# A conditioning group placed inside the norm ahead of the FFN of a hybrid decoder block, with a retuned table of places

## The chip, the cores and the metric

The kernel runs on one core of a Trainium2 chip, in float32 throughout. The metric is the device time of one execution in microseconds (us). A time of 1207.5 us is the median of three runs of the kernel before.

## The reference, cut to what matters

One decoder block for 256 tokens of width 2048. A vector `c` gives, through the matrix `w_ada` (2048 x 12288, 96 MB), six vectors of 2048 numbers ("adaLN"): a shift, a scale and a gate for the mixer (SH1, SC1, G1) and the same for the FFN (SH2, SC2, G2).

```python
mod = silu(c) @ w_ada + b_ada
sh1, sc1, g1, sh2, sc2, g2 = split(mod, 6)
h = modulate(rms_norm(x, norm1_g), sh1, sc1)            # h * (1 + scale) + shift
q, k, v, gb, gc, xt = split(h @ w_in, ...)              # 2048 x 6144
attn = attention(rms_norm(q), rms_norm(k), v)           # 8 heads, causal
conv = gb * causal_dwconv(gc * xt)                      # 3 taps
mixed = concat(rms_norm(attn), rms_norm(conv))
x = x + g1 * (mixed @ w_out)                            # 2048 x 2048
h2 = modulate(rms_norm(x, norm2_g), sh2, sc2)           # the norm ahead of the FFN
u_gate, u_up = split(causal_dwconv(h2 @ w_ffn_up), 2)   # 2048 x 11264
x = x + g2 * ((silu(u_gate) * u_up) @ w_ffn_down)       # 5632 x 2048
```

## The kernel before

**Matrices.** Every weight matrix is streamed in tiles of 1 MB (128 x 2048 floats) through five buffers, `raw`. SyncE issues the loads in a fixed order, the next one each time a buffer is given back (`load_next`). TensorE multiplies float32 by a split: ScalarE writes the rounded part `hi` of a tile (L225), VectorE the rest `lo` = raw - hi (L231), both with three buffers, and TensorE makes three products for each piece (hi with both parts of the activations, lo with one).

**Slots.** The program is a list of slots, one for each weight tile: 0 to 47 input projection, 48 to 63 output projection, from 64 (`N_OUT`) FFN up and down. In slot i the main loop at the end of the kernel issues, in program order: the split of the tile two slots ahead, the side work hung on the slot with `at(i, f, ...)` (a class number decides whether it stands before or behind the `lo` part, and a list `hi_late` whether the `hi` part stands before or behind it), the products of the slot, and then the `w_ada` tiles listed for the slot in `extra`. Each engine runs its instructions in this order; nothing is reordered later. `CFG` is the table of all these places.

**adaLN.** A group `[part, first chunk, width, on TensorE, first slot, span]` of `CFG['ada']` is a block of columns of `w_ada`. `Ada.consume` takes one 1 MB tile of it: on VectorE four or so multiply-adds (L287), or on TensorE (`pe` True) 16 matmuls a tile in four column quarters at once, which the profile counts in records of L281; a group of 512 columns has four tiles. Then `evac` copies the sum (ScalarE, L298), and `cols` turns it by four transposes (L314) into columns of the scale `A2` or the shift `B2`. Part 3 is SH2. Its chunks 8 to 11 are taken on TensorE in slot 63, all four tiles behind the last product of the output projection.

**The end of the mixer and the norm.** `evac_c(3)` adds the last quarter of the output projection to the residual x (VectorE, L454 and L456, twice: once for each 128 tokens). `tr_out(f)` turns the quarter f of the new x by eight transposes on TensorE (L489) and two copies on ScalarE (L492) into `x1T`. `norm2` squares the last quarter (ScalarE, L531, twice), makes the root of the mean (VectorE, ScalarE), writes the reciprocal into a diagonal `n2d` (VectorE, L537), spreads it over all partitions by one product with ones (`n2b`, TensorE, L539), copies it (L541) and makes from `x1T` the first eight chunks of h2 (VectorE L557, ScalarE L559, VectorE L562). `ss_part` sums the squares of the first three quarters (L498, L499, and a small root `pre`, L500, on ScalarE). The first FFN products (L662 with hi, L666 with lo) wait for the first chunk of h2.

**The start.** `ffn_cols` turns five small vectors by five transposes on TensorE (L167) and five copies on VectorE (L169), in slot 2.

Of the kernel before, what the change touches and what calls it, by code (L numbers as in the profile page):

```python
# [28 lines left out]

CFG = {'ada': [[3, 12, 512, False, 51, 12], [3, 0, 512, True, 58, 5], [0, 2, 256, False, 0, 7],
# [5 lines left out]
 'bufs': [43, 10, 5, 3, 2],  # L38
# [3 lines left out]
 'split': [4, 8],  # L42
 'segs': [8, 5, 5, 4],
 'heads': [35, 38, 38, 36, 41, 45, 43, 41],
 'head_steps': [1, 1, 2, 3, 4],
 'conv': [[1, 2, 1, 5, 4, 5, 7, 9], [2, 3, 3, 3, 2, 3, 2, 6]],
 'qk': [[1, 6], [2, 7]],
 'norms': [50, 55],
 'x1': 52,
 'fcols': 2,  # L50
 'hold': [1, 2, 0],
 'evac': [4, 0, 1],
 'sq': [4, 6, 2],
 'tr': [6, 7, 3],
 'part': 1,
 'up': [[1, 4], [1, 3], [0, 0], [2, 2]],
 'gate': [-21, -14, -2, -9],
 'cls': {'add': 0,
         'h2_rest': -1,
         'att_n': 1,  # L60
         'qk_norm': 0,
         'out_norm': -1,
         'cols': 0,
         'conv_q': -1,
         'att_q': 0,
         'up_gate': 2,
         'hold_a': 0,
         'spread': 1,
         'conv_m': 2,
         'ffn_cols': 2,  # L70
         'h_chunks': -1,
# [15 lines left out]
         'gate_down': 1,
         'conv_g': 0,
         'conv_c': 2,
         'evac_in': 0,  # L90
         'qk_root': 2,
         'evac_out': 1},
 'la': 2,
 'h_act': True,
 'h_lag': 1,
 'hi_late': [2, 3, 5, 6, 7, 8, 10, 12, 13, 15, 18, 27, 42, 44, 49, 50, 52, 53, 54, 56, 57, 63, 67, 68, 70, 75, 76,
# [3 lines left out]


@with_exitstack
def tile_block(
# [24 lines left out]
    def small(n, name):  # L128
        return sb.tile([P, n], F32, tag="small", bufs=16, name=name, padded_shape=[P, 32])
# [20 lines left out]
    vc, _ = rows("vc", [(by_p(c[0]), 16)])  # L150
# [212 lines left out]
    SLICES = [(0, 2), (2, 4), (4, 8), (8, 16)]  # L363

    def halves(v):
        return v[:, :256], v[:, 256:]
# [11 lines left out]
            mm(o, b, hi[:, k], start=False, stop=(last and k == nk - 1))  # L378

    def evac_in(f):  # L380
        for t in range(2):
# [17 lines left out]
    turns = []
    for (ka, kb), order in zip(SLICES, CFG["orders"]):  # L400
        if kb - ka == 2:
            turns += [((w + "0", w + "1"), ka, True, True) for w in order]
        else:
            turns += [((f,), k, k == ka, k + 4 == kb) for f in order for k in range(ka, kb, 4)]
    uses = {}
    for i, (fs, *_) in enumerate(turns):
        for f in fs:
            uses.setdefault(f, []).append(i)
    for i, (fs, k, first, last) in enumerate(turns):
        def near(f, d):  # L410
            u = uses[f]
            n = u.index(i) + d
            return 0 <= n < len(u) and abs(u[n] - i) <= 2

        def go(hi, lo, fs=fs, k=k, new=[not near(f, -1) for f in fs], end=[not near(f, 1) for f in fs]):
            m = 4 // len(fs)
            for h, f in enumerate(fs):
                mm_tok(f, hi[:, h::len(fs)], lo[:, h::len(fs)], [halves(hT[k + j]) for j in range(m)], m, new[h], end[h])

        slots.append((pair_load(k, fs[0]) if len(fs) == 2 else w_load(w_in, k, 4, [(COL[fs[0]] * 512, 512)]), 4, go))  # L420
        for f in fs:
            if not near(f, 1):
                at(len(slots), evac_in, f)
            if i == uses[f][-1]:
                at(len(slots), done.add, f)
                in_last[f] = len(slots)
    N_IN = len(slots)

# [466 lines left out]

# [148 lines left out]
    for i in range(len(slots)):  # L1044
        more = i + LA < len(slots)
        hi_late = i == N_OUT or i in CFG["hi_late"]
        if more and not hi_late:
            split_hi(slots[i + LA][1])
        todo = sorted(tasks.pop(i, []), key=lambda e: e[0])
# [12 lines left out]
        for g, r in extra.get(i, []):  # L1062
            g.consume(r)
# [33 lines left out]
```

## Time and profile before

| | |
|---|---|
| median of 3 runs (lowest to highest) | 1207.5 us (1207.37 to 1208.13) |
| the profiled execution | 1208.13 us, its span 1206.3 us |
| TensorE (PE) busy | 1174.2 us, 97% of the span |
| VectorE (DVE) busy | 916.8 us, 76% |
| ScalarE (ACT) busy | 616.9 us, 51% |
| bytes moved | 313.78 MB, 260 GB/s over the span |
| mean granted TensorE clock | 0.996 of full |

PE is the engine to look at: the span less its busy time is 32.1 us. Of the span, 87% of the chain of work that ended last is PE's own. The profiled execution is the slowest of the three, 0.63 us over their median.

### The profile page before, as it was taken

To read this page: it belongs to the slowest core of one execution; us is meant where nothing else is said; L and a number is where in the kernel's file an instruction comes from. 1 tells how busy PE (TensorE), PEld (TensorE's weight loads), DVE (VectorE), ACT (ScalarE), POOL (GpSimd) and SP (SyncE) were. 2 spreads that over 40 slices of the span, in tenths; PEclk is the share of its full clock that TensorE was granted. 3 is DMA by queue.
4 is the path that set the end of the run, shared out by engine and by line. 5 is a ranking of instruction groups with operands and counts; after the bars stand their busy time and mean duration, and the time that the engine had idled before them with its cause. 6 is when DMAs were issued, how large, how long until landed. Compare 5 with 4: busy or idle time off the path is not lost.

```text
span 1206.3 us, 15491 instructions
## 1 busy us (share of the span) xinstructions
PE 1174.2 (97%) x6041; PEld 965.1 (80%) x6041; DVE 916.8 (76%) x1099; ACT 616.9 (51%) x852; POOL 1.6 (0%) x9
## 2 busy tenths in 40 slices
PE   5899999999999998999999999999999999999998
PEld 3677788877777776888888888888888888888886
DVE  2789999997789896778888687766755667666776
ACT  5554347465765445555555344555434555345452
POOL 0000000000000000000000000000000000000000
PEclk9999999999999998999999999999999999999999
DMA  9999997999779997655576799554565564664542
GB/s 363 358 373 378 362 389 277 367 349 349 261 238 395 360 368 260 233 179 179 201 264 238 279 345 362 199 188 162 174 230 189 168 208 149 209 225 159 176 139 105
DMA packets 194925, 313.78 MB, mean 260 GB/s; under 512 B 6650, under 2 KB 105500, under 8 KB 194596
## 3 DMA queue, kind: packets, MB, share of 16 engines
q1 hardware_dynamic: 194160, 312.52, 72.8%
q8 instruction: 47, 0.77, 0.2%
q10 hardware_dynamic: 692, 0.28, 0.1%
q14 instruction: 26, 0.21, 0.0%
HBM read 310.67 MB, written 2.10 MB: 259 GB/s over the span
## 4 chain that ended last, share of the span: by engine, by line
PE 87%; DVE 6%; ACT 3%; DMA 2%; issue 1%; SPq 0%; ACTq 0%
PE z L662 27%; PE z L666 14%; DVE lo L231 2%; DVE ada L287 2%; PE ada L281 2%; DMA raw<-in_w_ada_dram 2%; ACT hi L225 2%; PE mk L376 1%; PE mq L376 1%; PE mq L378 1%; PE mq L377 1%; PE mk L377 1%; PE mk L378 1%; PE mg L376 1%; PE mg L378 1%; PE mg L377 1%
## 5 line engine op out<-in xcount | busy, mean ns | idle before, releaser
L231 DVE TENSOR_TENSOR lo<-raw,hi 128x2048 fp32r<-128x2048 f32 (+2 forms) x204 | 449.1, 2206 | 173.0 <-ACT hi L225 166.4
L225 ACT ACTIVATE hi<-raw 128x2048 fp32r<-128x2048 f32 (+2 forms) x204 | 376.1, 1847 | 344.9 <-PE z L662 104.7
L662 PE MATMUL z<-h,hi 128*128 128x512 f32 x1408 | 382.6, 396 | 2.1 <-DVE h L562 2.1
L662 PEld LDWEIGHTS z<-h,hi 128*128 128x128 f32 x1408 | 243.1, 189 | 37.8 <-issue 3.3
L666 PEld LDWEIGHTS z<-h,lo 128*128 128x128 f32 x1408 | 213.1, 189 | 27.9
L666 PE MATMUL z<-h,lo 128*128 128x256 f32 x1408 | 220.7, 281 | 0.0
L287 DVE SCALAR_TENSOR_TENSOR ada<-raw,csil,ada 128x1024 f32<-128x1024 f32 (+2 forms) x165 | 159.4, 968 | 4.5 <-DMA raw<-in_w_ada_dram 0.5
L579 DVE TENSOR_TENSOR ub<-z,ub 128x256 f32<-128x256 f32 x104 | 37.5, 417 | 33.0 <-ACT ub L576 33.0
L593 ACT ACTIVATE uy<-ub,fc,fc 128x256 f32<-128x256 f32 x88 | 45.7, 591 | 5.5 <-DVE uy L600 5.5
L281 PE MATMUL ada<-raw,crep 128*32 128x512 f32 (+1 forms) x320 | 37.1, 569 | 9.5 <-DMA raw<-in_w_ada_dram 9.5
L600 DVE SCALAR_TENSOR_TENSOR uy<-ub,fc,uy 128x254 f32<-128x254 f32 x88 | 42.5, 483 | 3.1
L609 ACT ACTIVATE gh<-uy 128x512 fp32r<-128x512 f32 x22 | 13.9, 632 | 58.1 <-DVE uy L607 58.1
L598 DVE SCALAR_TENSOR_TENSOR uy<-ub,fc,uy 128x255 f32<-128x255 f32 x88 | 42.1, 479 | 1.5 <-ACT uy L593 1.5
L576 ACT ACTIVATE ub<-z 128x256 f32<-128x256 f32 x104 | 33.1, 381 | 19.4 <-PE z L662 19.4
L603 ACT ACTIVATE uy<-uy 128x512 f32<-128x512 f32 x22 | 13.9, 631 | 44.7 <-DVE uy L600 44.7
L281 PEld LDWEIGHTS ada<-raw,crep 128*32 128x32 f32 x320 | 8.3, 116 | 25.6 <-issue 12.8
L376 PE MATMUL mc<-hi,h 128*128 128x512 f32 x64 | 26.0, 406 | 2.4 <-ACT pa_k L385 2.4
L610 DVE TENSOR_TENSOR gl<-uy,gh 128x512 fp32r<-128x512 f32 x22 | 15.2, 692 | 15.4 <-ACT gh L609 15.4
L376 PE MATMUL mg<-hi,h 128*128 128x512 f32 x64 | 26.1, 408 | 0.8 <-DVE v1c L169 0.8
L376 PE MATMUL mk<-hi,h 128*128 128x512 f32 x64 | 25.3, 396 | 0.7 <-ACT h L735 0.7
L378 PE MATMUL mv<-hi,h 128*128 128x512 f32 x64 | 25.0, 391 | 0.8 <-DVE h L738 0.8
L376 PE MATMUL mx<-hi,h 128*128 128x512 f32 x64 | 25.7, 401 | 0.0
(541 smaller groups left out, 1860.7 us busy)
## 6 DMA issues: line engine op xcount, KB each, us to landing
raw<-in_w_ada_dram SPq DMA_DIRECT2D x96, 1024.0 KB
raw<-in_w_ffn_up_dram SPq DMA_DIRECT2D x176, 512.0 KB
raw<-in_w_in_dram SPq DMA_DIRECT2D x48, 1024.0 KB
raw<-in_w_ffn_down_dram SPq DMA_DIRECT2D x24, 1024.0 KB
raw<-in_w_ffn_down_dram SPq DMA_DIRECT2D x24, 768.0 KB
raw<-in_w_out_dram SPq DMA_DIRECT2D x16, 1024.0 KB
xr<-in_x_dram SPq DMA_DIRECT2D x2, 1024.0 KB
x<-in_x_dram SPq DMA_DIRECT2D x8, 256.0 KB
```

What stands on the lines that cost most here:

```text
L225: act(hi[:, :nk], t[:, :nk], AF.Copy)
L231: V.tensor_tensor(out=lo[:, :nk], in0=t[:, :nk], in1=hi[:, :nk].bitcast(F32), op=ALU.subtract)
L281: mm(self.acc[q:q + 32, :], crep[:, i, :], t[:, j, :], start=(r == 0 and j < 4), stop=(r == self.tiles - 1 and j >= self.rows - 4), tile_p ...
L287: V.scalar_tensor_tensor(out=self.acc, in0=t[:, j, :], scalar=csil[:, i:i + 1], in1=self.acc, op0=ALU.mult, op1=ALU.add)
L376: mm(o, a, hi[:, k], start=(first and k == 0), stop=False)
L378: mm(o, b, hi[:, k], start=False, stop=(last and k == nk - 1))
L579: V.tensor_tensor(out=d, in0=zp[grp][ft][:, :256], in1=d, op=ALU.add)
L593: act(y, b, AF.Identity, bias=fcols[3][:, i:i + 1], scale=fcols[2][:, i:i + 1])
L598: V.scalar_tensor_tensor(out=y[:, 1:], in0=b[:, :255], scalar=fcols[1][:, i:i + 1], in1=y[:, 1:], op0=ALU.mult, op1=ALU.add)
L600: V.scalar_tensor_tensor(out=y[:, 2:], in0=b[:, :254], scalar=fcols[0][:, i:i + 1], in1=y[:, 2:], op0=ALU.mult, op1=ALU.add)
L662: mm(zp[grp][ft], hi[:, j, ft * P:(ft + 1) * P], h2T[k + j], start=k + j == ks[0], stop=k + j == ks[1] - 1)
L666: mm(zp[grp][ft][:, :256], lo[:, j, ft * P:(ft + 1) * P], h2T[k + j][:, :256], start=False, stop=False)
```

## The change

Three things. The group SH2, chunks 8 to 11, leaves the list of slots: three of its tiles are now consumed at the start of `norm2`, the fourth behind the product `n2b`, and its `evac` and `cols` go to slots 65 and 66. `tr_out(3)` moves from slot 64 to slot 65. And the table is retuned in many places: among them `ffn_cols` from slot 2 to 3, the second tile of the group `[1, 2]` from slot 2 to 3, the group `[4, 0]` from slots 49 and 50 to 49 alone, the group `[3, 0]` from slots 58 to 61 to 58 and 59, `ss_part` one slot earlier, and the FFN's side work (`gate`, `up`, the classes). The amount of work on each engine and the bytes are the same.

```diff
-         [4, 0, 512, True, 49, 2], ... [3, 8, 512, True, 63, 1],
-CFG = {'ada': [... [3, 0, 512, True, 58, 5], ... [1, 2, 256, True, 0, 4],
+CFG = {'ada': [... [3, 0, 512, True, 58, 2], ... [1, 2, 256, True, 0, 6],
+         [4, 0, 512, True, 49, 1], ...
+ 'fill': [[3, 8]],
+ 'fill_at': [0, 3, 1],
+ 'tr3': 1,
- 'fcols': 2,
+ 'fcols': 3,
- 'part': 1,
+ 'part': 0,
...
     def norm2():
-        assert {"tr0", "tr1", "tr2", "tr3"} <= done
+        assert {"tr0", "tr1", "ev3"} <= done
         m, q, r = small(2, "n2m"), small(2, "n2q"), small(2, "n2r")
+        for g, i in fill_a:
+            g.consume(i)
         for t in range(2):
             act(t2k("x1s"), x1[t, 3], AF.Square, accum_out=q[:, t:t + 1])
...
         p = bank("n2b")
         mm(p[:, :256], ones, d, start=True, stop=True)
+        for g, i in fill_b:
+            g.consume(i)
         rB.append(t1k("rB"))
...
     at(N_OUT, evac_c, 3)
-    at(N_OUT, tr_out, 3)
+    at(N_OUT + CFG["tr3"], tr_out, 3)
     at(N_OUT, norm2)
...
+    fill = []
+    for part, c0 in CFG["fill"]:
+        g = Ada(part, c0, 512, True)
+        fill += [(g, r) for r in range(g.tiles)]
+    n0, n1, n2 = CFG["fill_at"]
+    extra.setdefault(N_OUT - 1, []).extend(fill[:n0])
+    fill_a, fill_b = fill[n0:n0 + n1], fill[n0 + n1:n0 + n1 + n2]
...
     for i in range(len(slots)):
+        if i == N_OUT:
+            consume += [("a", g, r) for g, r in fill_a + fill_b]
         if i + LA < len(slots):
             consume.append(("w", i + LA))
```

The new lines shift the numbers of the file: L281, L376, L489, L531, L539, L662 before are L286, L380, L496, L540, L548, L673 in the changed kernel.

**TensorE at the norm.** Before, from the last product of the output projection to the first FFN product (`m('C', 3)1` is the last accumulator of that projection, `x1t` the turned x, `z` the FFN's accumulators; `x16` stands for 16 matmuls):

```order
L378 MATMUL m('C', 3)1_3687<-hi,mix_3071 128x512
L281 MATMUL ada_8_3789<-raw,crep 32x512 x16
L489 MATMUL x1t_3823<-ident,x_03_3202 128x128
L489 MATMUL x1t_3823<-ident,x_13_3210 128x128
...
L539 MATMUL n2b<-n2d,ones 128x256
L662 MATMUL z_0_3905<-h_0_3859,hi 128x512
```

and now, to the transposes behind the products of slot 64:

```order
L382 MATMUL m('C', 3)1_3727<-hi,mix_3088 128x512
L286 MATMUL ada_8_3798<-raw,crep 32x512 x12
L548 MATMUL n2b<-n2d,ones 128x256
L286 MATMUL ada_8_3798<-raw,crep 32x512 x4
L673 MATMUL z_0_3889<-h_0_3845,hi 128x512
...
L677 MATMUL z_3_3892<-h_3_3859,lo 128x256
L496 MATMUL x1t_3927<-ident,x_03_3270 128x128
```

The 16 matmuls of the group are now 12 ahead of `n2b` and 4 behind it, and the eight transposes stand behind 32 FFN products.

**ScalarE at the norm.** Before, from the split of tile 65 to the copy of `n2b` (`pre` is the small root, `x1T` the turned x, `x1s` the squares):

```order
L225 ACTIVATE hi<-raw 128x2048
L500 ACTIVATE pre<-ss_94 128x2
L492 ACTIVATE x1T_3828<-x1t_3823 128x512
L492 ACTIVATE x1T_3835<-x1t_3830 128x512
L531 ACTIVATE x1s,n2q<-x_03_3202 128x512
L531 ACTIVATE x1s,n2q<-x_13_3210 128x512
L533 ACTIVATE n2q<-n2m 128x2
L541 ACTIVATE rB<-n2b 128x256
```

and now:

```order
L507 ACTIVATE pre<-ss_94 128x2
L230 ACTIVATE hi<-raw 128x2048
L540 ACTIVATE x1s,n2q<-x_03_3270 128x512
L540 ACTIVATE x1s,n2q<-x_13_3278 128x512
L542 ACTIVATE n2q<-n2m 128x2
L552 ACTIVATE rB<-n2b 128x256
```

The two copies of the turned x no longer stand ahead of the squares; they come after the eight chunks of h2 and two splits.

**TensorE at slots 2 and 3.** Before, at the start of slot 2 (`pv_...` are the transposes of `ffn_cols`, `mc` and `mg` accumulators of the input projection):

```order
L378 MATMUL mc_380<-hi,h_255 128x512
L167 MATMUL pv_v1c<-ident,v_279 128x66
L167 MATMUL pv_fc_411<-ident,vf_287 128x88
L167 MATMUL pv_fc_415<-ident,vf_289 128x88
L167 MATMUL pv_fc_419<-ident,vf_291 128x88
L167 MATMUL pv_fc_423<-ident,vf_293 128x88
L376 MATMUL mg_427<-hi,h_251 128x512
```

and now, at the start of slot 3 (`mx` is the next accumulator):

```order
L382 MATMUL mg_422<-hi,h_255 128x512
L172 MATMUL pv_v1c<-ident,v_279 128x66
L172 MATMUL pv_fc_460<-ident,vf_287 128x88
L172 MATMUL pv_fc_464<-ident,vf_289 128x88
L172 MATMUL pv_fc_468<-ident,vf_291 128x88
L172 MATMUL pv_fc_472<-ident,vf_293 128x88
L380 MATMUL mx_476<-hi,h_251 128x512
```

The five transposes stand 24 products later, where a pass of the group `[1, 2]` stood before.

## Rows read from the trace of the kernel before

**Rows 1.** The page, first part: busy time of each engine, its share of the span, and its instructions.

```profile
PE 1174.2 (97%) x6041; PEld 965.1 (80%) x6041; DVE 916.8 (76%) x1099; ACT 616.9 (51%) x852; POOL 1.6 (0%) x9
```

**Rows 2.** Stretches of the span: from and to (us), length, busy time and instructions of PE, PEld, DVE, ACT and POOL, then the granted TensorE clock (1.00 is 2.4 GHz, 0.50 is 1.2 GHz), the DMA engines' share and GB/s.

```profile
0.00:30.00 30.00, 15.74 (x114) 9.85 (x115) 8.96 (x24) 16.40 (x24) 1.60 (x9) 1.00 0.97 363
...
100.00:250.00 150.00, 150.00 (x688) 120.58 (x687) 139.25 (x142) 75.60 (x144) 0.00 (x0) 1.00 0.94 351
...
450.00:462.00 12.00, 6.08 (x45) 2.33 (x43) 5.16 (x15) 3.79 (x10) 0.00 (x0) 0.87 1.02 354
...
600.00:900.00 300.00, 300.00 (x1521) 254.28 (x1520) 216.16 (x211) 143.75 (x149) 0.00 (x0) 1.00 0.70 245
900.00:1200.00 300.00, 300.00 (x1586) 257.61 (x1585) 201.56 (x223) 139.01 (x148) 0.00 (x0) 1.00 0.52 175
```

**Rows 3.** What PE's matmuls waited for, over the span: us in total, times, longest.

```profile
PE ada L281 <- DMA raw<-in_w_ada_dram: 9.5, 4, 6.9
...
PE n2b L539 <- DVE n2d L537: 3.8, 1, 3.8
...
PE z L662 <- DVE h L562: 2.1, 1, 2.1
...
PE mg L376 <- DVE v1c L169: 0.8, 1, 0.8
...
PE ssC L868 <- DVE sq L864: 0.7, 1, 0.7
```

**Rows 4.** The norm ahead of the FFN in order of time, all engines: start, duration, engine, line, operation, and in brackets the idle time before it and what ended it.

```profile
446.99 2.29 DVE L231 TENSOR_TENSOR lo<-raw,hi 128x2048 fp32r<-128x2048 f32 x1 [0.71 <-ACT hi L225]
...
449.91 0.39 PE L378 MATMUL m('C', 3)1_3687<-hi,mix 128*128 128x512 f32 x1
450.22 3.64 PE L281 MATMUL ada<-raw,crep 128*32 128x512 f32 x32
...
451.63 0.69 DVE L456 TENSOR_TENSOR x<-z,x 128x512 f32<-128x512 f32 x1
...
453.80 1.09 PE L489 MATMUL x1t<-ident,x 128*128 128x128 f32 x8
454.49 1.09 ACT L492 ACTIVATE x1T<-x1t 128x512 f32<-128x512 f32 x2 [4.70 <-PE x1t L489]
455.46 0.63 ACT L531 ACTIVATE x1s<-x 128x512 f32<-128x512 f32 x1
...
456.07 0.63 ACT L531 ACTIVATE x1s<-x 128x512 f32<-128x512 f32 x1
...
458.04 0.48 DVE L537 TENSOR_SCALAR n2d<-ident,n2r 128x128 f32<-128x128 f32 x2
...
458.67 1.08 PE L539 MATMUL n2b<-n2d,ones 128*128 128x256 f32 x2 [3.78 <-DVE n2d L537]
459.78 0.38 ACT L541 ACTIVATE rB<-n2b 128x256 f32<-128x256 f32 x1 [2.56 <-PE n2b L539]
...
461.89 2.05 PE L662 MATMUL z<-h,hi 128*128 128x512 f32 x4 [2.14 <-DVE h L562]
...
469.27 0.60 PE L314 MATMUL adac<-ident,adae 128*128 128x128 f32 x4
```

**Rows 5.** Shorter stretches, with the columns of rows 2.

```profile
42.40:45.80 3.40, 3.40 (x13) 2.72 (x12) 2.34 (x2) 3.29 (x5) 0.00 (x0) 0.50 1.07 392
...
270.00:275.00 5.00, 3.79 (x26) 2.40 (x23) 3.23 (x7) 0.83 (x1) 0.00 (x0) 1.00 1.04 399
...
458.80:461.90 3.10, 0.96 (x3) 0.27 (x3) 1.52 (x4) 1.29 (x3) 0.00 (x0) 0.50 1.07 389
461.90:465.60 3.70, 3.70 (x11) 3.12 (x12) 3.70 (x11) 2.32 (x5) 0.00 (x0) 0.50 0.93 328
465.60:469.20 3.60, 3.60 (x23) 3.17 (x22) 1.62 (x5) 3.23 (x5) 0.00 (x0) 1.00 0.01 3
```

**Rows 6.** PE alone in a stretch of the FFN, two rows of the same piece of work in neighbouring slots (columns of rows 4).

```profile
624.47 1.09 PE L662 MATMUL z<-h,hi 128*128 128x512 f32 x4
...
630.09 1.09 PE L662 MATMUL z<-h,hi 128*128 128x512 f32 x4
```

**Rows 7.** PE alone at four of its waits (columns of rows 4; the first is the wait ahead of the half clock near 42 us).

```profile
40.87 0.50 PE L376 MATMUL mc<-hi,h 128*128 128x512 f32 x1 [2.41 <-ACT pa_k L385]
...
48.77 0.50 PE L376 MATMUL mg<-hi,h 128*128 128x512 f32 x1 [0.83 <-DVE v1c L169]
...
72.82 0.50 PE L378 MATMUL mv<-hi,h 128*128 128x512 f32 x1 [0.82 <-DVE h L738]
...
271.57 1.06 PE L281 MATMUL ada<-raw,crep 128*32 128x512 f32 x8 [1.21 <-DMA raw<-in_w_ada_dram]
```

**Rows 8.** VectorE at the start, in order of time: a split, the copies of `ffn_cols` behind the first, and the chunk of h that PE waits for at 72.82.

```profile
46.29 2.29 DVE L231 TENSOR_TENSOR lo<-raw,hi 128x2048 fp32r<-128x2048 f32 x1 [1.55 <-ACT hi L225]
...
48.63 0.71 DVE L169 COPY fc<-pv_fc 128x88 f32<-128x88 f32 x4
...
72.34 0.76 DVE L738 TENSOR_TENSOR h<-hf,h 128x256 fp32r<-128x256 f32 x2
```

**Rows 9.** Slot 49: the two loads of SyncE and the two `w_ada` tiles of PE, in order of time.

```profile
355.87 3.89 SPq L258 DMA_DIRECT2D raw<-in_w_ada_dram  x2
358.27 1.92 PE L281 MATMUL ada<-raw,crep 128*32 128x512 f32 x16
```

More of the change, by code (lines that the diff above doesn't have):

```diff
@@ L28 @@
 SH1, SC1, G1, SH2, SC2, G2 = range(6)
-CFG = {'ada': [[3, 12, 512, False, 51, 12], [3, 0, 512, True, 58, 5], [0, 2, 256, False, 0, 7],
[5 rows of a table removed]
- 'bufs': [43, 10, 5, 3, 2],
[3 rows of a table removed]
+CFG = {'ada': [[3, 12, 512, False, 51, 12], [3, 0, 512, True, 58, 2], [2, 0, 1024, False, 24, 17],
[4 rows of a table added]
+ 'bufs': [43, 10, 5, 3, 2],
[6 rows of a table added]
+ 'fill': [[3, 8]],
+ 'fill_at': [0, 3, 1],
+ 'tr3': 1,
  'split': [4, 8],
  'segs': [8, 5, 5, 4],
- 'heads': [35, 38, 38, 36, 41, 45, 43, 41],
+ 'heads': [1, 4, 4, 2, 0, 4, 3, 0],
  'head_steps': [1, 1, 2, 3, 4],
- 'conv': [[1, 2, 1, 5, 4, 5, 7, 9], [2, 3, 3, 3, 2, 3, 2, 6]],
- 'qk': [[1, 6], [2, 7]],
+ 'conv': [[1, 2, 2, 5, 4, 6, 7, 8], [2, 3, 3, 3, 2, 3, 2, 6]],
+ 'qk': [[2, 6], [0, 7]],
  'norms': [50, 55],
- 'x1': 52,
- 'fcols': 2,
[L51 to L54, printed above, removed]
- 'part': 1,
[L56 to L59, printed above, removed]
+ 'x1': 54,
+ 'fcols': 3,
+ 'hold': [3, 2, 0],
+ 'evac': [4, 0, 0],
+ 'sq': [4, 6, 0],
+ 'tr': [5, 6, 1],
+ 'part': 0,
+ 'up': [[1, 3], [1, 3], [0, 0], [2, 2]],
+ 'gate': [-21, -14, -2, -11],
+ 'cls': {'add': 2,
+         'h2_rest': 0,
          'att_n': 1,
          'qk_norm': 0,
-         'out_norm': -1,
-         'cols': 0,
-         'conv_q': -1,
+         'out_norm': 0,
+         'cols': -1,
+         'conv_q': 1,
          'att_q': 0,
@@ L67 @@
          'hold_a': 0,
-         'spread': 1,
+         'spread': 2,
          'conv_m': 2,
@@ L77 @@
          'ss_part': 2,
-         'up_sum': -1,
+         'up_sum': 0,
          'sq_out': 1,
          'att_s': -1,
-         'tr_out': 0,
+         'tr_out': 1,
          'evac': 1,
          'qk_stat': 0,
-         'load_x': 2,
+         'load_x': 0,
          'att_t': 1,
          'att_o': 2,
-         'gate_down': 1,
+         'gate_down': 2,
          'conv_g': 0,
@@ L90 @@
          'evac_in': 0,
-         'qk_root': 2,
+         'qk_root': 0,
          'evac_out': 1},
@@ L95 @@
  'h_lag': 1,
- 'hi_late': [2, 3, 5, 6, 7, 8, 10, 12, 13, 15, 18, 27, 42, 44, 49, 50, 52, 53, 54, 56, 57, 63, 67, 68, 70, 75, 76,
[3 rows of a table removed]
+ 'hi_late': [2, 3, 4, 5, 6, 7, 8, 10, 12, 15, 18, 19, 27, 31, 42, 44, 49, 50, 52, 53, 54, 56, 57, 63, 67, 70, 71,
[3 rows of a table added]
 @with_exitstack
@@ L351, in tile_block @@
     done = set()
+    now = [0]
     hT = {}
@@ L361, in tile_block @@
            "x0": 10, "x1": 11}
-    SLICES = [(0, 2), (2, 4), (4, 8), (8, 16)]
     def halves(v):
@@ L380, in evac_in @@
     def evac_in(f):
+        if in_last.get(f) == now[0]:
+            done.add(f)
         for t in range(2):
@@ L396, in pair_load @@
         return issue
[L399 to L404, printed above, removed]
+    turns, upto = [], {}
+    for f, ka, kb in CFG["turns"]:
+        fs, step = ((f,), 4) if f in COL else ((f + "0", f + "1"), 2)
+        for g in fs:
+            assert upto.get(g, 0) == ka
+            upto[g] = kb
+        turns += [(fs, k) for k in range(ka, kb, step)]
+    assert len(upto) == 12 and set(upto.values()) == {16}
     uses = {}
-    for i, (fs, *_) in enumerate(turns):
+    for i, (fs, _) in enumerate(turns):
         for f in fs:
             uses.setdefault(f, []).append(i)
-    for i, (fs, k, first, last) in enumerate(turns):
+    for i, (fs, k) in enumerate(turns):
         def near(f, d):
@@ L424, in tile_block @@
             if i == uses[f][-1]:
-                at(len(slots), done.add, f)
                 in_last[f] = len(slots)
@@ L738, in h_chunks @@
                 V.tensor_tensor(out=hT[k][:, 256:], in0=ts[k], in1=hT[k][:, :256].bitcast(F32), op=ALU.subtract)
+    fill = []
[5 more added lines that the diff above has]
+    fill_a, fill_b = fill[n0:n0 + n1], fill[n0 + n1:n0 + n1 + n2]
+    for i, (g, r) in enumerate(fill):
+        if i >= n0 + n1 + n2:
+            extra.setdefault(N_OUT + (i - n0 - n1 - n2) // 2, []).append((g, r))
+        if r == g.tiles - 1:
+            a = N_OUT + 1 + max(0, (i - n0 - n1 - n2) // 2)
+            at(a, g.evac)
+            at(a + 1, g.cols)
+            ready_at.update({(g.part, g.c0 + k): a + 1 for k in range(4)})
     for part, c0, n, pe, a, span in CFG["ada"]:
@@ L888, in tile_block @@
         at(i + CFG["qk"][half][1], qk_norm, half)
+        n = i + CFG["qk"][half][1]
         for j in range(4):
@@ L891, in tile_block @@
             for i, f in zip([0] + CFG["head_steps"], (att_t, att_s, att_n, att_p, att_o, att_q)):
-                at(CFG["heads"][h] + i, f, h)
+                at(n + CFG["heads"][h] + i, f, h)
     at(CFG["norms"][0], out_norm, "A", ssA)
@@ L947, in tile_block @@
     for half in range(2):
-        xl, gl = in_last[f"x{half}"], in_last[f"g{half}"]
+        xl, gl = max(in_last[f"x{half}"], in_last[f"c{half}"]), in_last[f"g{half}"]
         o = CFG["conv"][half]
-        at(max(xl, in_last[f"c{half}"]) + o[0], conv_p, half)
+        at(xl + o[0], conv_p, half)
         at(xl + o[1], conv_c, half, 0)
@@ L1048, in tile_block @@
             split_hi(slots[i + LA][1])
+        now[0] = i
         todo = sorted(tasks.pop(i, []), key=lambda e: e[0])
```

24 rows, old and new, of the table CFG are left out of this document.

## The prediction

> **What bounds the kernel now.** I read the busy times first. TensorE (PE) works 1174.2 us of a span of 1206.3 us [rows 1]: 32.1 us without work are all that an order of instructions can win from waits, and what it loses shows there too. Next, where those 32.1 us lie. The table of stretches [rows 2] shows 14.26 us ahead of 30 us (30.00 less 15.74), when the first weights are still coming, 5.92 us at 450 to 462, and none at 100 to 250 and 600 to 1200. VectorE is at 139.25 of 150 us and the DMA engines at 0.94 in 100 to 250; at 600 to 1200 both have room. The list of PE's waits [rows 3] gives the names: `w_ada` tiles 9.5 us, 6.9 of it in one wait at the start, the product `n2b` 3.8 us, the first FFN product `z` 2.1 us, and pieces of 0.7 to 0.8 us for `mg`, `mv` and `ssC` [rows 3, 7]. Last the norm in order of time [rows 4], where the two large waits in the middle of the kernel stand next to each other.
>
> **The norm, step by step.** The last product of the output projection starts at 449.91 and ends at 450.30. PE then has the four adaLN tiles, 3.64 us, and the eight transposes, 1.09 us, to 454.89. VectorE has the last quarter of x ready at 452.32 (451.63 and 0.69), but ScalarE stands in front of the transposes: its queue holds the two copies of the turned x ahead of the squares, so it sits idle 4.70 us until PE has turned x, copies for 1.09 us, and squares at 455.46 and 456.07 [rows 4]. From the second square to `n2b` it is 2.60 us (456.07 to 458.67), from `n2b` to `z` 3.22 us (to 461.89).
>
> In the changed order no copy stands ahead of the squares. The second square can start when x is ready, at 452.32 and a handing over of some 0.15 us (`n2d` ends at 458.52, `n2b` starts at 458.67). `ss_part`, two small VectorE instructions, has moved ahead of the split of tile 65, and of the earlier ScalarE copies two are gone from the front of that split, so VectorE may come to x a little sooner: between 0 and 0.45 us, since the second half of x can't be begun before 450.30. I take 0.3. Then the second square starts at 452.2, `n2b` at 454.8, `z` at 458.0 with the durations of now. At 2.4 GHz `n2b` takes half of its 1.08 us, so `z` is at 457.5. That is 4.4 us earlier than 461.89; 3.6 us is the lower bound (no help from VectorE, `n2b` as slow as now), 4.6 the upper.
>
> The tiles cost PE no time here: 12 of 16 matmuls are three quarters of 3.64, so 2.73 us to 452.95; the fourth tile, 0.91 us, starts behind `n2b` at 455.3 and ends at 456.2, ahead of `z`. At half clock it would end near 457.7, still ahead of a `z` at 458.0. That cover is 0.3 to 1.3 us; were it gone, `z` would be late by what the tile overruns. The transposes, hidden now, are no longer: they stand behind slot 64's products, where PE has work, and cost their 1.09 us, a little less without the 0.1 us or so of start-up: 1.0. Their two copies on ScalarE come behind eight chunks of h2 and two splits, and only the chunks 12 to 15 of h2, wanted slots later, need them. Each consumed tile frees a buffer and lets SyncE issue one load; the fourth is freed some 2.3 us later than now (456.2 for 453.86). At 465.6 to 469.2 the DMA engines are at 0.01 [rows 5]: loads wait there for buffers and there is 3.6 us of room. So waits less moved work: 4.4 less 1.0, 3.4 us (2.6 to 3.6).
>
> **The clock.** The granted clock is 0.50 at 458.80 to 465.60, that is 1.2 GHz, after the idle time of 3.78 us [rows 4, 5]. Slot 64 takes 7.38 us from `z` to `adac` (461.89 to 469.27); an FFN slot at 2.4 GHz takes 5.62 us (624.47 to 630.09) [rows 6]. So the slow clock costs 1.76 us of products today. In the changed kernel PE idles 1.8 us ahead of `n2b` (452.95 to 454.8) and 1.2 to 1.3 us ahead of `z`. The trace has a wait of 2.41 us, at 40.87, behind which the clock was 0.50 for 3.40 us (42.40 to 45.80), and one of 1.21 us, at 271.57, in a stretch of 1.00 [rows 5, 7]. The new gaps lie between, but there are two of them with little between, so I take one short fall: the 3.40 us of the shorter case, of which part falls on the waits and the tile and some 2 us on products, which costs 1.0 us. Bounds: no fall, 0; a fall wholly on products, 1.7. Gain from the clock: 1.76 less 1.0, so 0.8 (0 to 1.8). The norm gives 3.4 and 0.8: 4.2 us (2.6 to 5.4).
>
> A rule speaks against taking the group apart. The Trainium skill, "Perfetto Trace Analysis", section Matmul Optimizations, says that matmuls should run back-to-back in batches, because the engine scales its power with its use; and "TensorE: Matmul & The Clock Gate", section HAM oscillation, says that idle time between bursts puts the array back to half its clock. By it the pieces ahead of and behind `n2b` don't hold the clock, and the total is that of my forecast; by the 1.21 us row alone it would be that of the first rival. The trace agrees for 2.41 and 3.78 us, and not for 1.21.
>
> **The start.** The transposes and copies of `ffn_cols` leave slot 2. PE waits 0.83 us for the first copy at 48.77 [rows 7]; that wait is gone, since a slot later VectorE's split is not in front of anything that PE needs at once. The transposes ran in the half-clock stretch of 42.40 to 45.80; now products fill it, so nothing is won there. VectorE gives the five copies, some 0.9 us (48.63 and 0.71 is their larger part), a later place. The next meeting is at 72.82, where PE waits 0.82 us for a chunk of h that VectorE makes at 72.34 [rows 7, 8]. The copies still lie ahead of it, but VectorE had idle time ahead of its split at 46.29, 1.55 us, so it may come 0 to 1.0 us sooner. Behind it, PE at 150.00 of 150 would keep a lead, but VectorE and DMA are nearly full [rows 2], and at 271.57 PE waits 1.21 us for a `w_ada` tile: a lead that the loads don't share is lost there. I take 0.4 us (0 to 1.0).
>
> **The other places.** Group `[4, 0]`: four tiles in slot 49. Two of them took 1.92 us (358.27), so the third is wanted at 360.2 and the last near 361. SyncE issued two loads at 355.87 over 3.89 us [rows 9]: the later tile's load depends on a buffer freed just before. A wait of 0 to 0.7 us, since its load is already under way; I take 0.2. Group `[3, 0]` has two tiles in slots 58 and 59 each, again the load of the third behind the use of the first: 0 to 1.0, I take 0.2. `ssC` waits 0.7 us for a square; some of VectorE's work ahead of it stands elsewhere: a gain of 0 to 0.4, I take 0.2. The tile of `[1, 2]` a slot later, heads, convolution, `evac` and `gate` places and the classes move work of VectorE and ScalarE at places where PE shows no wait (100 to 250 and 600 to 1200); the cover is the third `hi`/`lo` buffer and, at 900 to 1200, an idle VectorE for 98 of 300 us and an idle ScalarE for 161 [rows 2]. They cost nothing unless a split comes more than about a slot, 5.62 us, late. Sum of this part: -0.2 us (-1.7 to 0.4).
>
> **The sum.** 4.2, 0.4 and -0.2 are 4.4 us. The profiled execution took 1208.13, which gives 1203.7 us; it is 0.63 above the median of 1207.5, and against the median the sum is 1203.1 us.
>
> **Rivals.** (1) The clock doesn't fall: the 1.21 us row speaks for it, two gaps in a row against it. It adds 1.0 to the gain: 1202.1 us. (2) New waits on loads take part of it: the doubled tiles at slots 49, 58 and 59 at their upper bounds, 1.7 us, with no gain at `ssC` and none kept from the start; PE's longest wait for a tile in the middle of the kernel, 1.21 us, shows that such loads do come late. 4.2 less 1.7: 1205.0. (3) The change doesn't do what it says: the squares are held by something else in ScalarE's queue. The split `hi` of tile 65 stands there, now directly ahead of them; should a late load hold it to 454.7, the second square would be at 455.5 rather than 456.07, `z` 0.6 us earlier, and the transposes would take 1.0 back: about 1207.5, no change. Against it: VectorE's `lo` of that tile started at 446.99 [rows 4], so `hi` was done by then, and no later load than now is put ahead of it. (4) Slower: the FFN's side work. 600 us at 5.62 are some 107 slots with a split each; if the new classes and the list `hi_late` put longer pieces ahead of `lo`, so that PE waits 0.1 us in each, that is 10.7 us, and the time is 1213.8. It decides the sign from 0.04 us a slot on (4.4 by 107). Against it: PE at 300.00 of 300, VectorE idle for 84 and 98 us of 300 [rows 2]; for it: the waits would come from an order that this trace can't show.
>
> **Chances.** Forecast 0.38, rival 1 0.27, rival 2 0.15, rival 3 0.08, rival 4 0.07; 0.05 are left for all else. What a measurement of this kernel can tell from no change is about 0.2%, 2.4 us: faster is under 1205.1. The forecast, rival 1 and two thirds of rival 2 are faster, with a little of the rest: 0.77. Same: the rest of rival 2, rival 3: 0.14. Slower: rival 4 and a part of the rest, 0.09. The range is 1200.7 (the norm's upper bound, 5.4, with the start's 1.0 and `ssC`) to 1206.0 (the norm's lower bound of 2.6 with a loss of 1.1 at the tiles); rivals 3 and 4 lie outside it.
>
> **What would show it.** In the changed kernel's trace: the squares near 452 with no idle time behind the transposes; `n2b` near 454.8 and `z` near 457.5 after the same last product, with waits of about 1.8 and 1.2 us; the clock of the stretch from `n2b` on; the transposes behind slot 64's products at about 1 us; the wait at `mg` gone and that at 271 larger or not; waits of `ada` on DMA near 360 and 423; PE still full from 600 to 1200. I am wrong if the squares still wait for ScalarE's queue, or if PE shows waits behind 470.

## The result, and the profile after

The changed kernel takes 1198.17 us (median of four runs, 1196.96 to 1199.11); before took 1207.43 us in the runs beside it (1206.25 to 1208.13). The ratio is 0.9924, 95% interval 0.9907 to 0.9941: 9.3 us faster, where 4.4 were forecast, and 2.5 us below the range. A second round of the unedited kernel gave 1199.3 us (five runs, 1196.42 to 1200.05) and a ratio of 0.9933 (0.9919 to 0.9947). The nine runs together have a median of 1198.74, a spread of 3.6 us, so a difference of under a microsecond is read here from profiles, not from times.

The page of the profiled execution (1196.96 us), first part, against [rows 1]:

```profile
PE 1169.1 (98%) x6041; PEld 962.5 (81%) x6041; DVE 917.4 (77%) x1099; ACT 614.1 (51%) x850; POOL 1.6 (0%) x9
```

The span is 1195.2 us: PE's time without work fell from 32.1 to 26.1 us, and its busy time by 5.1 us with the same 6041 instructions, much of it time at the slow clock: 10.2 us of the profile before ran at 0.50 (42.40 to 45.80 and 458.80 to 465.60, [rows 5]), and 3.4 us of this one, in slot 1 (the row by itself). The stretches, against [rows 2]:

```profile
34.00:38.00 4.00, 4.00 (x20) 2.63 (x13) 1.80 (x1) 3.29 (x2) 0.00 (x0) 0.57 1.02 406
```

```profile
0.00:30.00 30.00, 16.10 (x122) 10.37 (x123) 9.84 (x25) 17.30 (x24) 1.60 (x9) 1.00 0.98 366
...
100.00:250.00 150.00, 150.00 (x688) 120.52 (x687) 139.99 (x149) 77.56 (x149) 0.00 (x0) 1.00 0.95 352
...
450.00:462.00 12.00, 10.95 (x68) 9.50 (x65) 10.32 (x18) 9.03 (x13) 0.00 (x0) 1.00 0.90 315
...
600.00:900.00 300.00, 300.00 (x1519) 254.26 (x1518) 213.03 (x201) 139.10 (x140) 0.00 (x0) 1.00 0.70 241
```

The FFN is as full as it was. PE's waits, against [rows 3]:

```profile
PE ada L286 <- DMA raw<-in_w_ada_dram: 10.2, 3, 7.1
...
PE n2b L548 <- DVE n2d L546: 1.5, 1, 1.5
...
PE mv L382 <- DVE h L749: 1.4, 1, 1.4
PE z L673 <- DVE h L573: 1.1, 1, 1.1
...
PE ssC L896 <- DVE sq L892: 0.7, 1, 0.7
```

`n2b` and `z` waited 5.9 us together and wait 2.6 now; the wait of `mg` is gone. The norm in order of time, against [rows 4]:

```profile
443.94 0.39 PE L382 MATMUL m('C', 3)1_3727<-hi,mix 128*128 128x512 f32 x1
444.26 2.78 PE L286 MATMUL ada<-raw,crep 128*32 128x512 f32 x24
...
445.31 0.69 DVE L463 TENSOR_TENSOR x<-z,x 128x512 f32<-128x512 f32 x1
446.04 0.63 ACT L540 ACTIVATE x1s<-x 128x512 f32<-128x512 f32 x1 [0.67 <-DVE x L463]
...
448.55 0.70 PE L548 MATMUL n2b<-n2d,ones 128*128 128x256 f32 x2 [1.50 <-DVE n2d L546]
449.18 1.06 PE L286 MATMUL ada<-raw,crep 128*32 128x512 f32 x8
...
451.30 1.20 PE L673 MATMUL z<-h,hi 128*128 128x512 f32 x4 [1.05 <-DVE h L573]
...
457.00 1.04 PE L496 MATMUL x1t<-ident,x 128*128 128x128 f32 x8
```

Counted from the end of the last product (443.94 and 0.39 is 444.33; 450.30 before), `n2b` starts at 4.2 us (8.4 before) and `z` at 7.0 us (11.6). But the last product itself is 6.0 us earlier than before: more than half of the profiled difference of 11.1 us was won ahead of the norm.

To see where, the products of both kernels can be lined up by number: a slot of the projections has 24, an FFN up slot 32, whatever stands between them. The table gives the length of four stretches, from the first product of one slot to the first of another, in each kernel's profile (us):

| kernel | slots 1 to 4 | 4 to 38 | 49 to 63 | 63 to 67 |
|---|---|---|---|---|
| before | 23.74 | 205.16 | 91.96 | 36.35 |
| changed | 19.47 | 205.62 | 91.28 | 30.79 |
| changed, again | 21.26 | 205.05 | 91.07 | 30.80 |
| e1, norm undone | 19.51 | 205.35 | 91.22 | 36.91 |
| e2, tiles ahead | 19.89 | 205.88 | 91.38 | 33.58 |
| e3, x turned ahead | 20.78 | 204.99 | 91.10 | 32.18 |
| e4, before with norm | 23.77 | 205.14 | 92.01 | 31.41 |
| e6, start undone | 23.60 | 205.14 | 91.09 | 30.80 |
| e8, tiles apart | 20.72 | 205.05 | 91.92 | 30.87 |
| e9, before with start | 24.39 | 205.04 | 92.04 | 36.11 |
| e11, with slot 4 too | 22.19 | 204.99 | 92.02 | 37.13 |
| e12, before with both | 19.51 | 205.70 | 91.96 | 31.42 |
| e13, slot 4 undone | 23.17 | 205.00 | 91.02 | 30.81 |
| e14, x turned in the gap | 20.53 | 205.99 | 91.06 | 30.00 |

From slot 67 to its end, before takes 725.4 us more and the changed kernel 725.7: nothing was won or lost in the FFN. At slots 38 to 49 the profile of before alone has 88.94 us and all others 87.3 to 88.0: its wait of 1.21 us at 271.57 [rows 7] belongs to that execution, since e4, e9 and e11 have the same table there and no such wait. Some 1.5 us of the 6.0 ahead of the norm are therefore chance.

### The profile page after: what moved, and what is told of

Same layout as the page of the kernel before. It is cut to its first block, busy times and chain, and to the rows that moved or that the text cites. A ratio compares the mean times of both kernels' runs of the same rounds, so it can differ in the third digit from the quotient of the medians.

```text
span 1195.2 us, 15484 instructions
## 1 busy us (share of the span) xinstructions
PE 1169.1 (98%) x6041; PEld 962.5 (81%) x6041; DVE 917.4 (77%) x1099; ACT 614.1 (51%) x850; POOL 1.6 (0%) x9
## 4 chain that ended last, share of the span: by engine, by line
PE 93%; DVE 3%; DMA 3%; ACT 1%; issue 0%; SPq 0%; ACTq 0%
PE z L673 27%; PE z L677 14%; DMA raw<-in_w_ada_dram 3%; PE ada L286 2%; PE mc L380 1%; PE mc L381 1%; PE mc L382 1%; PE mx L380 1%; PE mq L380 1%; PE mv L382 1%; PE mg L380 1%; PE mk L380 1%; PE mg L382 1%; PE mx L382 1%; PE mg L381 1%; PE mx L381 1%
## 5 line engine op out<-in xcount | busy, mean ns | idle before, releaser
L673 PE MATMUL z<-h,hi 128*128 128x512 f32 x1408 | 381.3, 395 | 1.1 <-DVE h L573 1.1
L673 PEld LDWEIGHTS z<-h,hi 128*128 128x128 f32 x1408 | 242.2, 189 | 36.7 <-DVE h L573 2.0
L286 PE MATMUL ada<-raw,crep 128*32 128x512 f32 (+1 forms) x320 | 36.5, 566 | 10.2 <-DMA raw<-in_w_ada_dram 10.2
L620 ACT ACTIVATE gh<-uy 128x512 fp32r<-128x512 f32 x22 | 13.9, 632 | 58.1 <-DVE uy L618 58.1
L587 ACT ACTIVATE ub<-z 128x256 f32<-128x256 f32 x104 | 32.2, 382 | 11.6 <-PE z L673 11.6
L286 PEld LDWEIGHTS ada<-raw,crep 128*32 128x32 f32 x320 | 8.4, 113 | 26.4 <-issue 14.3
L380 PE MATMUL mc<-hi,h 128*128 128x512 f32 x64 | 26.2, 409 | 0.0
L380 PE MATMUL mk<-hi,h 128*128 128x512 f32 x64 | 25.3, 396 | 0.7 <-ACT h L746 0.7
L380 PE MATMUL mx<-hi,h 128*128 128x512 f32 x64 | 25.8, 402 | 0.0
L380 PE MATMUL mg<-hi,h 128*128 128x512 f32 x64 | 25.5, 398 | 0.0
```

What stands on the lines that cost most here:

```text
L286: mm(self.acc[q:q + 32, :], crep[:, i, :], t[:, j, :], start=(r == 0 and j < 4), stop=(r == self.tiles - 1 and j >= self.rows - 4), tile_p ...
L380: mm(o, a, hi[:, k], start=(first and k == 0), stop=False)
L673: mm(zp[grp][ft], hi[:, j, ft * P:(ft + 1) * P], h2T[k + j], start=k + j == ks[0], stop=k + j == ks[1] - 1)
```

## The experiments

**The norm, put back and put in.** e1 is the changed kernel with `'fill_at': [4, 0, 0]` and the last quarter of x turned ahead of the norm:

```diff
-    at(N_OUT + CFG["tr3"], tr_out, 3)
+    tasks.setdefault(N_OUT, []).append((0, tr_out, (3,)))
     at(N_OUT, norm2)
```

> The changed kernel with its norm put back: all four tiles of the group behind slot 63, the last quarter of x turned ahead of the norm; all else as changed. Theory A (the two profiles, lined up product by product, show PE's lead growing from 6.0 to 11.4 us across the norm): the norm is worth 5.4 us, so this kernel is 5.4 us slower than the changed one, near 1203.6 us, with a wait of 3.8 us at n2b and a clock of 0.50 behind it. Rival B: the norm is worth only its idle time less the transposes, 3.6 us, and the clock falls in both by chance: near 1201.8 us.

Measured: 1204.11 us, ratio to before 0.9978 (0.9970 to 0.9987); 5.4 us slower than the nine runs of the changed kernel. Its waits, and the granted clock (columns of rows 2; the clock is the third number from the end):

```profile
PE n2b L548 <- DVE n2d L546: 3.7, 1, 3.7
PE z L673 <- DVE h L573: 2.1, 1, 2.1
```

```profile
452.00:456.00 4.00, 1.60 (x3) 0.91 (x4) 2.08 (x7) 1.39 (x4) 0.00 (x0) 0.50 1.07 391
456.00:460.00 4.00, 4.00 (x12) 3.25 (x12) 4.00 (x11) 2.60 (x6) 0.00 (x0) 0.50 0.81 287
```

The waits of before are back, and the clock of 0.50 with them. Theory A holds. It also says that the rest of the change is worth about 3 us without the norm.

e4 is the kernel before with the norm's edit alone.

> The kernel before with the edit of the norm alone (three tiles at the start of the norm, one behind n2b, x turned a slot later), its table otherwise untouched. Theory A: 5.4 us faster than before, near 1202.0 us. Rival B: 3.6 us, near 1203.8 us. If most of the gain comes from elsewhere and the norm's edit needs the retuned table (the small sums still stand behind the split of tile 65), under 3 us.

Measured: 1202.24 us, ratio 0.9960 (0.9948 to 0.9972), 4.9 us faster than before beside it. The stretch from slot 63 to 67 is 31.4 us against 30.8 in the changed kernel. Here the two small VectorE instructions of `ss_part` still stand between the split of tile 65 and x, and x is ready 2.0 us behind the last product where it was 1.7. Theory A.

**Which part of the norm's edit.** e2 has `'fill_at': [4, 0, 0]` alone, e3 the turn ahead of the norm alone (the diff above).

> The changed kernel with all four tiles behind slot 63, ahead of the norm, as before; the last quarter of x is still turned a slot later. Theory A (the copies of the turned x ahead of the squares are what made the norm late; the place of the tiles matters through the clock alone): the squares start when x is ready, n2b at the same time as in the changed kernel, PE idles 0.6 us ahead of n2b and 2.0 us ahead of z, the clock stays up: the changed kernel's time within 0.5 us. Rival B (the pieces behind n2b keep the clock up): z comes at the same time but the clock falls, 1 to 1.7 us slower than the changed kernel.

Measured: 1200.36 us, ratio 0.9950 (0.9937 to 0.9963). Here is PE at the norm of e2, and two stretches of the granted clock, first of e2 and then of the changed kernel:

```profile
444.60 3.64 PE L286 MATMUL ada<-raw,crep 128*32 128x512 f32 x32
448.89 0.70 PE L548 MATMUL n2b<-n2d,ones 128*128 128x256 f32 x2 [0.65 <-DVE n2d L546]
451.64 2.07 PE L673 MATMUL z<-h,hi 128*128 128x512 f32 x4 [2.05 <-DVE h L573]
```

```profile
452.00:456.00 4.00, 4.00 (x12) 3.30 (x12) 4.00 (x11) 2.60 (x6) 0.00 (x0) 0.50 1.06 396
456.00:460.00 4.00, 4.00 (x20) 3.48 (x19) 2.51 (x3) 2.39 (x3) 0.00 (x0) 0.77 0.98 346
```

```profile
452.00:456.00 4.00, 4.00 (x25) 3.51 (x24) 3.97 (x11) 2.61 (x6) 0.00 (x0) 1.00 1.07 396
456.00:460.00 4.00, 4.00 (x29) 3.65 (x29) 2.53 (x2) 4.00 (x4) 0.00 (x0) 1.00 0.91 323
```

`z` starts 7.0 us behind the last product in both, so the place of the tiles does not change when the norm is done. It changes how the idle time is cut: 0.65 and 2.05 us in e2, 1.50 and 1.05 in the changed kernel. With the wait of 2.05 us the clock went to 0.50, and the stretch to slot 67 took 2.8 us more. Rival B holds in the profile; in the times it is 1.1 to 1.6 us. The mean granted clock of the five runs (each known to 0.001) is 0.9964, and 0.9984 over the nine of the changed kernel. That is an estimated 4.9 us more at half clock (0.0020 of 1198 us, twice), where the profile has 6.8 at the norm, so the fall need not be as long in every execution.

> The changed kernel with the last quarter of x turned ahead of the norm again (eight transposes, two copies ahead of the squares); the tiles stay three at the start of the norm and one behind n2b. Theory A (ScalarE's queue: the squares wait for the copies, the copies for the transposes, which now wait for x alone and not for the tiles): x is ready 1.7 us behind the last product, transposes 1.0, copies to 3.7, second square 4.4 us behind it instead of 1.7, so n2b and z 2.4 us later than in the changed kernel, the transposes' 1.0 us hidden again: net 1.4 us slower, and up to 1.7 more if the clock falls. Rival B (the tiles ahead of the transposes were the cause, not the copies): within 0.5 us of the changed kernel.

Measured: 1198.86 us, ratio 0.9931 (0.9917 to 0.9945), in time no different from the changed kernel, as rival B has it. In the profile the stretch from slot 63 to 67 is 1.4 us longer, as theory A has it: the copies stand ahead of the squares again. Why the times don't show it stays open.

```profile
447.35 1.09 ACT L499 ACTIVATE x1T<-x1t 128x512 f32<-128x512 f32 x2 [5.74 <-PE x1t L496]
448.32 0.63 ACT L540 ACTIVATE x1s<-x 128x512 f32<-128x512 f32 x1
448.93 0.63 ACT L540 ACTIVATE x1s<-x 128x512 f32<-128x512 f32 x1
```

Against the changed kernel the tiles' place alone costs 2.8 us of the stretch (e2), the copies' place alone 1.4 (e3), both together 6.1 (e1): with the tiles also ahead of the transposes, the squares wait for PE, and the idle time is in one piece.

**The start.** e6 is the changed kernel with `'fcols': 2` and `[1, 2, 256, True, 0, 4]`.

> The changed kernel with the five transposes of the small vectors back in slot 2 and the second tile of the group [1, 2] back in slot 2. Theory A (the start keeps a lead of 3.6 us to 263 us in the profiles, of which 1.9 us were there before the first product and so are no doing of the table): 1.7 us slower than the changed kernel, near 1199.9 us. Rival B (the lead is all that one run's own luck at the start): 1198.2 us, no change. Rival C (all 3.6 us are the table's): 1201.8 us.

Measured: 1200.33 us, ratio 0.9947 (0.9934 to 0.9960): 1.6 us slower than the nine runs of the changed kernel, theory A; by the profile 2.3 to 4.1 us at slots 1 to 4, lost for good. Its wait for the first small copy is twice the one in [rows 3]:

```profile
PE mg L380 <- DVE v1c L174: 1.7, 1, 1.7
```

e9 puts the same two places into the kernel before.

> The kernel before with those two places of the start alone as in the change (transposes of the small vectors in slot 3, second tile of the group [1, 2] in slot 3). Theory A: 1.7 us faster than before, near 1205.7 us, and the lead at 263 us is kept to the end. Rival B: no change, 1207.4 us. Rival C: 3.6 us, near 1203.8 us.

Measured: 1206.51 us, ratio 0.9999 (0.9988 to 1.0010): no gain, rival B by the time. But the cause is not the one that I had in mind. PE at slot 3 of e9:

```profile
55.04 0.50 PE L376 MATMUL mx<-hi,h 128*128 128x512 f32 x1 [1.79 <-DVE v1c L169]
```

The wait has moved from `mg` to `mx`. What differs from the changed kernel is one number in the list `hi_late`: slot 4. With it, ScalarE copies the first pair of `mx` accumulators out ahead of the split of tile 6; without it, ScalarE first waits for the load of that tile. This is ScalarE in the changed kernel, and then with that number taken out (e13, below):

```profile
49.81 1.28 ACT L391 ACTIVATE pa_x<-mx 128x512 f32<-128x512 f32 x2
```

```profile
59.16 1.92 ACT L230 ACTIVATE hi<-raw 128x2048 fp32r<-128x2048 f32 x1 [8.91 <-DMA raw<-in_w_in_dram]
```

In e13 the copies come behind that split, from 60.99 us on. So the second pair of `mx` accumulators gets the banks of the first pair in the one program; in the other it gets those of the small transposes and waits for VectorE's copies. e11 is e9 with that number, e13 the changed kernel without it, and e12 e4 with all three places of the start:

```diff
- 'hi_late': [2, 3, 5, ...
+ 'hi_late': [2, 3, 4, 5, ...
```

> The kernel before with three places of the start as in the change: transposes of the small vectors in slot 3, second tile of the group [1, 2] in slot 3, and slot 4 in the list hi_late, so that ScalarE's copies of the x accumulators stand ahead of the split of tile 6. Theory A (without the third place the wait for the first small copy, 1.7 to 1.8 us at full clock, only moves from mg to mx, since mx takes the bank of that copy; with it mx takes the banks of the x accumulators): no wait on v1c, PE 2.5 to 3 us ahead at slot 4, kept to the end: 1204.2 us. Rival B (the start is lost again behind slot 36): 1206.8 us.

> The changed kernel with slot 4 taken out of the list hi_late, that one number alone. Theory A: PE waits about 1.8 us at mx for the first small copy (DVE v1c), the lead of the start shrinks by 2.5 to 3 us at slot 5 and never comes back: near 1201.5 us. Rival B (the place of the transposes is what counts): no change, near 1198.9 us.

> The kernel before with the edit of the norm and those three places of the start, nothing else of the retuned table. Theory A (start 2.5 to 3, norm 5 to 5.5, the rest of the table under 1 us): 1199.2 us, within 1 us of the changed kernel. Rival B (the rest of the table carries 2 us or more): 1201 us or more.

Measured: e11 1204.44 us, ratio 0.9984 (0.9976 to 0.9993), 2.6 us faster than before beside it. e13 1200.05 us, ratio 0.9946 (0.9933 to 0.9959), with the wait back; in time 1.3 us slower than the nine runs, which lies between theory A and rival B, in the profile 1.9 to 3.7 us at slots 1 to 4.

```profile
PE mx L380 <- DVE v1c L174: 1.8, 1, 1.8
```

e12 1198.92 us, ratio 0.9940 (0.9926 to 0.9953): the norm and three numbers make the kernel before as fast as the changed one. By the waits all three are theory A, and by the times e11 and e12; the rest of the table is worth no more than the times can tell.

**The doubled tiles.** e8 is the changed kernel with `[4, 0, 512, True, 49, 2]` and `[3, 0, 512, True, 58, 5]`.

> The changed kernel with the group [4, 0] over slots 49 and 50 and the group [3, 0] over slots 58 to 61 again, as before. Theory A (the doubled tiles cost a wait of 0.7 us near 357 and nothing is won there; what the profiles show of a smaller lead at slots 50 and 59 to 62 is only that PE has done more tiles by then): within 0.5 us of the changed kernel. Rival B (taking the tiles early clears VectorE and the loads ahead of the norm): 1 us slower or more.

Measured: 1199.48 us, ratio 0.9935 (0.9922 to 0.9948): 0.7 us slower than the nine runs, between theory A and rival B. By the profile the tiles apart cost 0.6 to 0.9 us between slots 49 and 63 (91.92 against 91.28 and 91.07), as much as in before. A tile (four matmuls of the program, eight in the profile's records; the 16 matmuls are those of a group of four tiles) takes 1.06 us alone in before, two together 1.92 in the changed kernel, and four together 3.64 in its second profile (e10):

```profile
414.65 1.06 PE L281 MATMUL ada<-raw,crep 128*32 128x512 f32 x8
```

```profile
409.30 1.92 PE L286 MATMUL ada<-raw,crep 128*32 128x512 f32 x16
```

```profile
353.70 3.64 PE L286 MATMUL ada<-raw,crep 128*32 128x512 f32 x32
```

Four single tiles taken as two pairs (`[3, 0]`) save 0.4 us, two pairs taken as one four (`[4, 0]`) 0.2. In the first profile of the changed kernel that four took 3.87 us, so there a tile came some 0.2 us late. What is left, 0.2 to 0.3 us, stays open.

**The changed kernel once more**, unedited:

> The changed kernel once more, unedited, for a second profile and more times. In the first profile of it PE reached its first product 1.9 us earlier than before (25.4 against 27.3 us), with the same instructions ahead of it. Theory A (that is the run's own start, in which the clock came up earlier, and 2 us of the first profile's lead is chance): some executions start near 27.3 us and take 2 us longer; median near 1198.6 us. Rival B (it belongs to the changed order): all start near 25.4 us, and the median stays near 1197.5 us.

Measured: 1199.3 us. In this profile the first product starts at 27.25 us as before, not at 25.42: theory A, in that the start of an execution varies by 2 us. Its price of 2 us does not hold: this execution took 1197.31 us and the first profile 1196.96, and slot 1 begins at 34.3 to 35.2 us in all fourteen profiles, whenever the first product started. Slot 4 begins at 55.6 us here, against 58.1 to 59.0 in e4, e6, e9 and e13, which lack one or more of the three places (58.5 before). Over slots 1 to 4 the nine profiles that have all three take 19.5 to 22.2 us, mean 20.4, the other five 23.2 to 24.4, mean 23.7. Some of the fourteen have a stretch at half clock there; those without one differ as much, 19.5 to 21.3 us (e3, e8, e10, e12) against 23.6 and 23.8 (e6, e4). So the lead is the table's.

**A version beyond.** PE idles 1.50 us ahead of `n2b`, and the eight transposes cost 1.04 us behind slot 64. e14 puts them into that gap and leaves their copies where they are:

```diff
...
         for g, i in fill_a:
             g.consume(i)
+        tr_pe(3)
         for t in range(2):
             act(t2k("x1s"), x1[t, 3], AF.Square, accum_out=q[:, t:t + 1])
...
```

(`tr_pe` is the part of `tr_out` that issues the transposes; `tr_out` keeps the copies.)

> The changed kernel with the eight transposes of the last quarter of x between the three tiles and n2b, where PE idles 1.5 us; their two copies stay in slot 65, behind the chunks of h2. Theory A (the transposes, 1.0 us, fit into that idle time, and only their copies were in the squares' way): n2b and z as early as in the changed kernel, the 1.0 us behind slot 64 gone: 1 us faster, near 1197.9 us. Rival B (transposes in the gap don't keep the clock up, or their banks hold the first FFN products): z later or the clock at 0.50, no gain or up to 1.7 us slower.

Measured: 1197.04 us (1196.66 to 1200.71), ratio 0.9923 (0.9911 to 0.9934). The stretch from slot 63 to 67 is 30.0 us, 0.8 less than the changed kernel's, theory A:

```profile
448.07 1.09 PE L497 MATMUL x1t<-ident,x 128*128 128x128 f32 x8
449.64 0.70 PE L556 MATMUL n2b<-n2d,ones 128*128 128x256 f32 x2 [0.47 <-DVE n2d L554]
```

It has the lowest median of all, but its interval overlaps that of the changed kernel.

## Why the prediction was wrong

**The norm: right in its mechanism, short in the clock.** `n2b` was forecast 4.5 us behind the last product (454.8 less 450.3) and came at 4.2; `z` at 7.2 and came at 7.0; the idle times at 1.8 and 1.2 and came at 1.50 and 1.05; the transposes at 1.0, and took 1.04. Behind the last product `z` came 4.6 us earlier than before; less 1.04 for the transposes that is 3.6 us, where 3.4 were told. The step that failed is "I take one short fall": the clock stayed at 1.00, as rival 1 had it. Slots 63 to 67 show 5.6 us (36.35 to 30.79), a little above the upper bound of 5.4, where I took 4.2. The 2.0 us beside the 3.6 are in the main the slow products of slot 64 that are gone, where I took 0.8 from the clock. The step rested on one row, the wait of 2.41 us behind which the clock fell. That row was no measure: at the same place a wait of 2.69 us left the clock at 1.00 in e4 and in e10.

The rule of the Trainium skill that I set against the change, "Perfetto Trace Analysis", section Matmul Optimizations, asks for matmuls back to back in batches. Here the tiles in one batch lost the clock, in the one profile of e2, and the same tiles in two pieces kept it, in four profiles (the two of the changed kernel, e6, e13). The section of the Trainium skill that I set beside it, "TensorE: Matmul & The Clock Gate", section HAM oscillation, is about one long wait for data in every pass of a loop. That two short gaps would lose the clock was my own reading of it, and the runs don't bear it out.

**The start: wrong, and the larger error.** I took 0.4 us, with 1.0 as the bound; it gave 1.3 to 3.3 us by the four timed pairs (the changed kernel against e13 and e6, e11 against before, e12 against e4) and 3.3 by the profiles. Three steps failed. The first is the reason in "that wait is gone, since a slot later VectorE's split is not in front of anything that PE needs at once": e9 and e13 show that the wait only moves, to `mx`, unless slot 4 is in `hi_late`; I had not followed which copy frees the bank. The second is its price of 0.83 us, from one row [rows 7] behind a stretch at half clock (42.40 to 45.80), in which PE was late itself. In e4 `mg` starts at the same 48.8 us, but the clock was 1.00 from 30 to 60 us, and PE waited 1.7 us for the same copy. It waited 1.7 us in e6 too, and at `mx` 1.8 us in e9 and e13:

```profile
48.76 0.50 PE L376 MATMUL mg<-hi,h 128*128 128x512 f32 x1 [1.70 <-DVE v1c L169]
```

The third is "a lead that the loads don't share is lost there". From slot 4 to 38 all fourteen profiles take 205.0 to 206.0 us, so of a lead of 3.3 us in the mean 3.0 were left after 200 us of nearly full DMA queues. What was lost, up to 1.0 us, was mostly lost at the wait of `mv` for h, 0.8 us before, 1.4 in the changed kernel and 1.8 in e14. The wait at 271.57 on which I rested this was not of the program, but of that one execution.

**The doubled tiles: wrong in sign.** I charged 0.4 us for waits on loads and the upper bound of rival 2 was 1.7. Of such waits the profile after has some 0.2 us, at slot 49, and the second profile none; the stretch became 0.6 to 0.9 us shorter by the profiles (e8), a gain that I had not looked for, although the rows of before had tiles of 1.92 us for two and 3.64 for four.

**Rivals 3 and 4.** The squares start with x (446.04, VectorE done at 446.00), and the FFN shows no wait behind `z`. `ssC` still waits 0.7 us, so the 0.2 us there were nothing.

With the measured terms the sum is 5.6, some 2.5 and 0.8, about 9 us, and the medians show 9.3.

## What to carry to other kernels

A wait's length in one profile is what was left after the waiting engine's own lateness: look for what else made it late (a slow clock, a wait just before) before taking the row as the price. When a wait on a buffer or bank is to be moved away, follow which earlier user the new taker inherits. A lead won early need not be lost to full queues: here, where each load is issued when a buffer comes free, nine tenths of it lasted through 200 us; no run here has another order of issue. And one row with a slow clock behind a wait is no price for the next wait: look for the same wait in a second execution.

## What the runs showed of the hardware that I had not expected

At the norm the granted clock stayed at 1.00 in the nine profiles in which no single wait of PE was longer than 1.95 us, and fell to 0.50 in the five that have one of 2.05 us or more (before, e1, e2, e9, e11). So it looks as if the length of the longest piece of idle time decided. Near 41 us it did not. There, at the wait of `mc`, the clock fell to 0.50 with waits of 2.41 us (before), 2.52 (e9) and 1.89 (e11), and stayed at 1.00 with waits of 2.06 to 2.69 us in e3, e8, e6, e4 and e10. This is e4, against the first rows of [rows 7] and [rows 5]:

```profile
41.08 0.50 PE L376 MATMUL mc<-hi,h 128*128 128x512 f32 x1 [2.69 <-ACT pa_k L385]
```

```profile
42.00:46.00 4.00, 3.81 (x21) 2.98 (x20) 2.68 (x2) 4.00 (x7) 0.00 (x0) 1.00 1.08 411
```

What else decides is not shown by these runs. And the same program begins its first product at 25.4 us in one execution and at 27.2 in another, with the same instructions ahead of it; by slot 1 the difference is gone, so it does not explain the spread of the times, 3.6 us in nine runs.
